# A two-layer block of attention, pooling, S5 scan and gating: another layout of the scan, the readout operators on VectorE, another order of input blocks

## The chip, the cores and the metric

The kernel runs on one core of one Trainium2 chip. The metric is the device time in microseconds of one execution; lower is better. The core has TensorE (matrix products; PE in the views), VectorE (DVE), ScalarE (ACT), GpSimd (POOL), SyncE (SP, which mostly issues DMAs) and 16 DMA engines.

## The reference, cut to what matters

Two layers. Each normalises and modulates its input, projects it once, and hands parts of the projection to four parallel groups (latent attention, pooling mixer, S5 state space, spatial gating), whose outputs are gated, joined and projected back. 1,024 latent and 256 context tokens, width 1,024; the second layer computes outputs for latent tokens only.

```python
h = _ln(x) * (1.0 + scale) + shift
ckv, kr, s5_in, cq, pool_in, su, sv, g = jnp.split(h @ p['w_in'], IN_SPLITS, axis=-1)
...
for d, rev in enumerate((False, True)):
    disc = _s5_discretise(p['lam_re'][d], p['lam_im'][d], p['log_dt'][d],
                          p['s5_b_re'][d], p['s5_b_im'][d])
    hc_r, hc_i = _s5_scan(u_c, disc, rev, None)
    i_end = 0 if rev else nc - 1
    hl_r, hl_i = _s5_scan(u_l, disc, rev, (hc_r[i_end], hc_i[i_end]))
    y_l = y_l + _s5_readout(hl_r, hl_i, p['s5_c_re'][d], p['s5_c_im'][d]).reshape(b, n, BRANCH_W)
...
y = (jnp.concatenate([att_l, pool_l, s5_l, sgu_l], axis=-1) * jax.nn.silu(g)) @ p['w_out']
x_new = (_ln(ALPHA * x + gate * y) * p['ln_g'] + p['ln_b']).astype(x.dtype)
```

The scan is a complex, diagonal recurrence h = a h + b u over all tokens, in both directions, for 16 groups of 64 states.

## The kernel before

**The S5 path.** Tokens are taken in 160 slots of 8, so that the recurrence runs over slots with the 8th power of a, and everything inside a slot is a matrix product. `s5_operators` builds three things per layer from the parameters: the scan-input operators W (on VectorE, function `outer` with engine V, stored to `Ed`), the products inside a slot (kernel K, on TensorE, stored to `Kd`), and the readout operators R (function `outer` with engine P, that is on GpSimd, stored through the tile `bldR` to `Rd`). Their buffers are tiles named op. `s5_states` multiplies the loaded operators (tile Eld) with the tokens and puts the result into the tile H through ScalarE. H holds, for each of two directions, eight pairs of groups, the real and the imaginary part, 161 positions side by side.

`s5_scan` runs in place on H. The 160 positions are five segments of 32; all five are stepped at once, so a step touches positions 32 apart, that is 128 bytes. A step is, for each direction, one multiplication of 160 columns (128 partitions) and two additions of 80, all on VectorE, 31 steps. A table of powers of a is made on GpSimd before. Then a prefix adds the carry of one segment to the next: five small operations per segment and direction, and five larger ones, which stand on GpSimd for three of the four segments of direction 1 (constant PFIX) and else on VectorE. Last an exchange moves half of H to the other partitions, through DRAM: `Xd<-H`, then `H<-Xd`, both issued by GpSimd's queue. `s5_readout` multiplies H by R (tile Rld) and the tokens by M (copied from `Kd`) on TensorE.

**The input blocks.** The input projection is cut into blocks of 128 output columns: gate(i), pl(i) for pooling, su(i) for the spatial unit. For each, SP loads the weight (tile wraw), ScalarE makes its rounded part (whi), VectorE the remainder (wlo), and TensorE does 24 products per chunk of tokens: two with whi and one with wlo for each of eight slices. Layer 0 has three chunks (512, 512, 256 tokens), layer 1 two of 512. Loaded weights, modulation weights (wmod) and operators (Eld, M, Rld) share a ring of three buffers. VectorE evicts gate blocks with one multiplication (G).

**The order.** A list of items per layer sets the program's order: blocks, the states, and the pooled mix. Each block `more(block, n)` advances side work (generators of the operators and of the scan) by a few steps between its chunks; `step(1000)` and `advance(side, 100)` finish side work. Inside that order a scheduler places instructions per engine. Pooling: `pool_mix` forms the window sums of one pooled block, for b = 0 on GpSimd and for b = 1 on VectorE; TensorE then multiplies by w_pool (tp_pool), VectorE evicts. `sgu_prep` loads and transposes the spatial weights (sgw, tp_sgup) in one piece behind gate(4). In attention, for each head and block of queries, VectorE forms maxima (mx), two differences of queries (QA, QB, by `go("m4")`) and a row.

All element-wise operations go through helpers, so their line is the helper's: L131 two-tensor operations, L144 tensor and scalar, L148 both. L152 to L154 are the three products of an input block.

## Time and profile before

| | before |
|---|---|
| median of 3 runs | 1434.23 us (1432.74 to 1434.94) |
| profiled execution | 1430.7 us |
| its span, first to last instruction | 1428.9 us |
| mean granted TensorE clock | 0.950 of 2.4 GHz |
| TensorE busy | 1252.1 us (88%) |
| VectorE busy | 932.5 us (65%) |
| GpSimd busy | 554.7 us (39%) |
| ScalarE busy | 467.6 us (33%) |

A row of a timeline gives start and duration of an instruction, engine, line, operation, the tiles it writes and reads, its shape, and in brackets the idle time of the engine before it with what ended it. A duration is printed with its overlap to the next instruction, so that the distance of two starts is the better price. `x4` means four such instructions in a row, whose duration is that of all. The first layer's scan stretch lies at about 84 to 352 us, the second's at about 820 to 1073 us.

### The profile page before, as it was taken

The page shows a single profiled execution, that of the slowest core. Times are in us where ns is not written, and L with a number is a line of the kernel's source. Part 1 is how long each engine was busy: PE and PEld are TensorE (multiplying, and loading weights), DVE is VectorE, ACT ScalarE, POOL GpSimd, SP SyncE. Part 2 cuts the span into 40 slices and gives each one's busy share as a digit, 9 for nine tenths or more (in the row PEclk, how much of TensorE's full clock was granted, in tenths as well). Part 3 has the DMA queues.
Part 4 walks back from the last instruction along what each step waited for, and adds up shares of the span by engine and source line. Part 5 has one row for each costly group of instructions (what it writes and reads, how often), then busy time and mean ns, then how long its engine had stood idle before and what let it go on. Part 6 is the DMA issues. An engine that isn't in the chain of part 4 may idle for free.

```text
span 1428.9 us, 19998 instructions
## 1 busy us (share of the span) xinstructions
PE 1252.1 (88%) x7556; PEld 962.6 (67%) x7556; DVE 932.5 (65%) x1812; ACT 467.6 (33%) x879; POOL 554.7 (39%) x580
## 2 busy tenths in 40 slices
PE   3877994999999998999999869987599998998997
PEld 1555773779878766666777647765488786665685
DVE  7685399642543566767798882599517456767666
ACT  2341130121244644445243322301213454544300
POOL 2467230500102254665444592224101136756443
PEclk9887997999999989999999979998889999999999
DMA  9435322476320100014123444412662020000421
GB/s 322 135 94 177 115 85 75 117 199 151 83 57 19 45 23 1 1 42 133 48 74 103 100 140 158 138 45 59 135 161 66 11 60 23 30 2 16 150 101 73
DMA packets 124677, 127.31 MB, mean 89 GB/s; under 512 B 40908, under 2 KB 98724, under 8 KB 124582
## 3 DMA queue, kind: packets, MB, share of 16 engines
q1 hardware_dynamic: 118886, 111.86, 26.8%
q0 software_dynamic: 2880, 9.54, 2.8%
q10 hardware_dynamic: 2816, 4.65, 0.9%
q8 instruction: 59, 0.97, 0.3%
q14 instruction: 36, 0.29, 0.1%
HBM read 97.47 MB, written 25.94 MB: 86 GB/s over the span
## 4 chain that ended last, share of the span: by engine, by line
PE 51%; DVE 29%; POOL 6%; issue 6%; DMA 4%; ACT 3%; SPq 1%; DVEq 0%; POOLq 0%; ACTq 0%
PE mm_out L1637 7%; PE mm_sc L1332 6%; PE mm_in L154 6%; PE mm_in L152 6%; PE mm_in L153 6%; DVE H L131 5%; DVE stmp L131 3%; DVE z L148 3%; DVE acc L131 2%; PE av L1415 2%; DVE op L131 2%; PE mm_sc L1374 1%; POOL op L131 1%; DMA M<-Kd 1%; DVE xres L145 1%
## 5 line engine op out<-in xcount | busy, mean ns | idle before, releaser
L154 PE MATMUL mm_in<-hT,wlo 128*128 128x512 f32 (+1 forms) x696 | 264.9, 381 | 26.0 <-DVE wlo L131 26.0
L153 PE MATMUL mm_in<-hT,whi 128*128 128x512 f32 (+1 forms) x696 | 265.1, 381 | 5.0 <-POOL hT L131 2.5
L152 PE MATMUL mm_in<-hT,whi 128*128 128x512 f32 (+1 forms) x696 | 269.0, 388 | 0.4 <-ACT whi L638 0.4
L154 PEld LDWEIGHTS mm_in<-hT,wlo 128*128 128x128 f32 x696 | 136.8, 197 | 53.6 <-DVE wlo L131 28.7
L1637 PE MATMUL mm_out<-wo,yh 128*128 128x512 f32 x576 | 164.2, 398 | 1.8 <-DVE wo L131 1.7
L152 PEld LDWEIGHTS mm_in<-hT,whi 128*128 128x128 f32 x696 | 136.6, 197 | 36.9 <-issue 14.2
L153 PEld LDWEIGHTS mm_in<-hT,whi 128*128 128x128 f32 x696 | 136.5, 196 | 31.4 <-POOL hT L131 5.3
L1637 PEld LDWEIGHTS mm_out<-wo,yh 128*128 128x128 f32 x576 | 107.3, 188 | 29.9 <-DVE wo L131 3.3
L638 ACT CAST whi<-wraw 128x1024 fp32r<-128x1024 f32 x38 | 42.6, 1121 | 194.6 <-PE mm_in L153 146.8
L131 DVE TENSOR_TENSOR wlo<-wraw,whi 128x1024 fp32r<-128x1024 f32 x38 | 58.0, 1530 | 68.0 <-ACT whi L638 61.7
L131 DVE TENSOR_TENSOR acc<-acc,mm_sc 128x512 f32<-128x512 f32 x108 | 74.2, 687 | 42.3 <-PE mm_sc L1332 31.2
L131 POOL TENSOR_TENSOR psum<-pE 128x512 f32<-128x512 f32 (+1 forms) x36 | 47.4, 1318 | 124.2 <-ACT pE L1393 124.1
L1637 PE MATMUL mm_out<-wo,yl 128*128 128x512 f32 x288 | 93.1, 395 | 0.3 <-POOL yl L131 0.3
L131 POOL TENSOR_TENSOR psum<-psum,pL 128x512 f32<-128x512 f32 x64 | 83.2, 1300 | 6.4 <-ACT pL L1393 1.5
L131 DVE TENSOR_TENSOR H<-H,stmp 128x80 f32<-128x80 f32 x248 | 74.6, 355 | 0.8
L144 POOL TENSOR_SCALAR rs_z<-mv_z 128x1 f32<-128x1 f32 x18 | 18.5, 1029 | 119.9 <-DVE mv_z L1669 119.9
L144 POOL TENSOR_SCALAR srs<-smv 128x1 f32<-128x1 f32 x18 | 5.6, 310 | 152.6 <-DVE smv L1065 152.6
L1637 PEld LDWEIGHTS mm_out<-wo,yl 128*128 128x128 f32 x288 | 54.2, 188 | 13.4 <-POOL yl L131 0.8
L131 DVE TENSOR_TENSOR stmp<-a,H 128x160 f32<-128x160 f32 x124 | 53.3, 462 | 14.6 <-POOL pws L131 7.2
L1393 ACT ACTIVATE pE<-mm_sc 128x512 f32<-128x512 f32 x55 | 30.7, 595 | 95.0 <-PE mm_sc L1374 73.7
L1621 ACT CAST yh<-G 128x1024 fp32r<-128x1024 f32 x18 | 18.9, 1052 | 115.1 <-PE mm_out L1637 113.8
L1788 ACT ACTIVATE G<-mm_in 128x512 f32<-128x512 f32 (+1 forms) x40 | 22.2, 555 | 104.1 <-PE mm_in L154 104.0
(361 smaller groups left out, 2789.8 us busy)
## 6 DMA issues: line engine op xcount, KB each, us to landing
wmod<-in_w_mod_dram SPq DMA_DIRECT2D x48, 512.0 KB, 4.3
wraw<-in_w_in_dram SPq DMA_DIRECT2D x36, 512.0 KB, 4.1
wor<-in_w_out_dram SPq DMA_DIRECT2D x16, 512.0 KB, 3.5
s5u<-Sd SPq DMA_DIRECT2D x8, 640.0 KB, 7.3
xd<-z SPq DMA_DIRECT2D x10, 512.0 KB, 2.7
xin<-in_x_dram SPq DMA_DIRECT2D x8, 512.0 KB, 7.6
Ed<-E ACTq DMA_DIRECT2D x16, 256.0 KB, 3.0
Rd<-bldR POOLq DMA_DIRECT2D x16, 256.0 KB, 3.9
```

Of the source, the lines that this page charges most:

```text
L131: return e.tensor_tensor(out=out, in0=a, in1=b, op=op)
L144: return e.tensor_scalar(out=out, in0=a, scalar1=s1, scalar2=None, op0=op0)
L148: return V.scalar_tensor_tensor(out=out, in0=a, scalar=s, in1=b, op0=op0, op1=op1)
L152: T.matmul(out, lhsT=ahi, rhs=bhi, start=start, stop=False)
L153: T.matmul(out, lhsT=ahi, rhs=blo, start=False, stop=False)
L154: T.matmul(out, lhsT=alo, rhs=bhi, start=False, stop=stop)
L638: copy(hi, raw)
L1332: T.matmul(out, lhsT=K[:, e, 128 * kt_:128 * kt_ + 128], rhs=Q[:, f], start=(x == 0 and y == 0), stop=False, skip_group_check=True)
L1393: S.activation(out=p, in_=ps, func=AF.Exp, scale=QSCALE)
L1415: T.matmul(st[v][64 * h:64 * h + 64, 0:n], lhsT=Vt[:, BANKS[i // 2][i % 2], 64 * head:64 * head + 64], rhs=st[v, h]["pt"][i // 2][:, n * ( ...
L1637: T.matmul(a[1][nh], lhsT=y[u][:, k, :], rhs=self.W[k][:, v, 512 * nh:512 * nh + 512], start=(k == 0 and u == 0 and v == 0), stop=(k == KC ...
L1788: S.activation(out=G[ci][:, b, :], in_=ps, func=AF.Silu)
```

## The change

**Readout operators.** The calls of `outer` for R leave GpSimd and the loop over directions. They follow behind the W and K parts, on VectorE, with two buffers (`R` and `R2`, once GpSimd's op1). GpSimd keeps the DMAs `Rd<-bldR`.

**Scan.** H is laid out with the five segments side by side: position of step i and segment s is 5 i + s, 165 positions; direction 1 is stored reversed, so both directions take the same step. A step is one multiplication of 320 columns and two additions of 160. The power table is made on VectorE. The prefix makes first all carries (20 small operations of both directions together and a copy), then 16 operations of 8 x 31 x 4 = 992 columns on VectorE; PFIX is gone. ScalarE writes H, and TensorE reads H in the readout, with a step of 20 bytes.

**Pooling.** `pool_mix` is on VectorE for both blocks.

**Order.** pl(1) and mix(1) follow gate(2) (in layer 1 su(0)), ahead of su(1) and gate(3); before, they stood behind the end of the side work. The side work of the scan is finished behind gate(4) instead of ahead of pl(1). `sgu_prep` is cut in two: loads and transposes ahead of gate(4), the products and copies behind it.

**Attention.** `go("m4")`, which has the two differences of queries, follows the row operations instead of standing ahead of them.

```diff
-NPOS = 161
+NPOS = 165
-PFIX = (1, 2, 3)
...
-            Rv = R.rearrange("p (r c q) -> p r c q", r=2, c=4)
             for c in (slice(0, 4), slice(4, 8)):
                 k0, step = ((7, -1), (0, 1))[d]
                 outer(V, tv_, ld, k0, step, [Bb[:, ri, 8 * d:8 * d + 8, :] for ri in range(2)], c, [w[:, c] for w in W], 1)
-
-                k0, step = ((1, 1), (8, -1))[d]
-                outer(P, tp_, ld, k0, step, [CT[:, ri, 8 * d:8 * d + 8, :] for ri in range(2)], c,
-                      [Rv[:, ri] for ri in range(2)], -1)
-                for ri in range(2):
-                    P.dma_start(Rd[l][:, c, 2 * d + ri, :], Rv[:, ri])
                 yield
-            yield
...
+        for d in range(2):
+            for i, c in enumerate((slice(0, 4), slice(4, 8))):
+
+                k0, step = ((1, 1), (8, -1))[d]
+                Rv = (R, R2)[i].rearrange("p (r c q) -> p r c q", r=2, c=4)
+                outer(V, tv_, 2 * l + d, k0, step, [CT[:, ri, 8 * d:8 * d + 8, :] for ri in range(2)], c,
+                      [Rv[:, ri] for ri in range(2)], -1)
+                for ri in range(2):
+                    P.dma_start(Rd[l][:, c, 2 * d + ri, :], Rv[:, ri])
+                yield
...
         for i in range(1, SEG):
...
+            x = tmp[:, 320 * (i % 2):320 * (i % 2) + 64 * NSEG].rearrange("p (x k o s) -> p x k o s", x=16, k=2, o=2)
+            mul(V, x.rearrange("p x k o s -> p (x k) o s"),
+                a8l.rearrange("p x k o -> p (x k) o").unsqueeze(3).to_broadcast([128, 32, 2, NSEG]),
+                states_at(NSEG * i, [[NPOS, 32], [0, 2], [1, NSEG]]))
+            h = states_at(NSEG * i + NSEG, [[2 * NPOS, 16], [NPOS, 2], [1, NSEG]])
             for k in range(2):
...
+                add(V, h, h, x[:, :, k])
             yield
...
+        for d in range(2):
+            re, im = (T2[:, c, 8 * d:8 * d + 8, 0:w].unsqueeze(3).to_broadcast([128, 8, w, NSEG - 1]) for c in range(2))
+            for o in range(2):
+                own, other = (states_at((16 * d + y) * NPOS + 1, [[2 * NPOS, 8], [0, w], [1, NSEG - 1]]) for y in (o, 1 - o))
+                cur = states_at((16 * d + o) * NPOS + NSEG + 1, [[2 * NPOS, 8], [NSEG, w], [1, NSEG - 1]])
+                mul(V, m, re, own)
+                add(V, cur, cur, m)
+                mul(V, m, im, other)
+                tt(V, cur, cur, m, ALU.add if o else ALU.subtract)
+                yield
...
-                    T.matmul(o, lhsT=R_[:, 1, :], rhs=H[:, 1, pr, g, 1:1 + nr], start=False, stop=False)
+                    T.matmul(ov, lhsT=R_[:, 1, :], rhs=spread(H[:, 1, pr, g, NSLOT - 1:NSLOT], [[-1, nr // SEG], [-NSEG, SEG]]),
+                             start=False, stop=False)
...
-        e = V if b else P
+        e = V
...
-                go("m4")
                 vals(v, w, k, 1)
                 rows(v, h)
+                go("m4")
...
-        items += [more(gate(2), 3)] + ([more(su(0), 3)] if last else []) + [more(su(1), 3), more(gate(3), 3)]
-        items += [lambda: step(1000), lambda: advance(side, 100), more(pl(1), 3), mix(1), more(gate(4), 3)]
-        items += [lambda: step(1000), lambda: advance(side, 100), lambda: sgu_prep(l), begin(s5_readout(l, last))]
+        items += [more(gate(2), 3)] + ([more(su(0), 3)] if last else []) + [mixed, more(pl(1), 3), mix(1), more(su(1), 3)]
+        items += [more(gate(3), 3), mixed, lambda: next(prep), more(gate(4), 3), lambda: next(prep), lambda: step(1000)]
+        items += [begin(s5_readout(l, last))]
```

Three places of the order. First VectorE in layer 0's operators, before; op0 to op4 are the operator buffers, wlo the remainders of weight blocks, dd a part of K:

```order
L131 TENSOR_TENSOR wlo_1002<-wraw_997,whi_1001 128x1024
L131 TENSOR_TENSOR op0_766<-lamT_543,op4_770 128x512
L131 TENSOR_TENSOR wlo_1006<-wraw_999,whi_1005 128x1024
L131 TENSOR_TENSOR op2_768<-op0_766 128x512
L131 TENSOR_TENSOR op0_766<-lamT_543,op4_770 128x512
L620 COPY dd_914<-kt_1116 128x32
L131 TENSOR_TENSOR op0_766<-lamT_543,op4_770 128x512
L131 TENSOR_TENSOR op3_769<-op0_766 128x512
L131 TENSOR_TENSOR op0_766<-lamT_543,op4_770 128x512 x2
L131 TENSOR_TENSOR op2_768<-op0_766 128x512
L131 TENSOR_TENSOR op0_766<-lamT_543,op4_770 128x512 x2
L131 TENSOR_TENSOR wlo_1197<-wraw_1009,whi_1196 128x1024
```

And the same place of VectorE after; the last three of these rows belong to the readout operators:

```order
L130 TENSOR_TENSOR wlo_998<-wraw_991,whi_997 128x1024
L130 TENSOR_TENSOR op2_768<-op0_766 128x512
L130 TENSOR_TENSOR op0_766<-lamT_543,op4_770 128x512 x2
L609 COPY dd_914<-kt_1067 128x32
L130 TENSOR_TENSOR op3_769<-op0_766 128x512
L130 TENSOR_TENSOR op0_766<-lamT_543,op4_770 128x512 x2
L130 TENSOR_TENSOR op2_768<-op0_766 128x512
L130 TENSOR_TENSOR op0_766<-lamT_543,op4_770 128x512 x2
L130 TENSOR_TENSOR op3_769<-op0_766 128x512
L130 TENSOR_TENSOR op0_766<-lamT_543,op4_770 128x512 x2
L130 TENSOR_TENSOR bldR_912<-op0_766 128x4x8x16
L130 TENSOR_TENSOR op0_766<-lamT_543,op4_770 128x512 x2
```

The operators that TensorE transposes next (op2, op3) and the weight remainders keep their order; 24 readout instructions per layer now stand behind them on VectorE, with one wlo among them in layer 0.

Second TensorE in layer 0 where it takes up the first pooled block, before; mm_in_1959 is a chunk of su(1), tp_pool the pooled products, pv the window sums, mm_mod a modulation product:

```order
L153 MATMUL mm_in_1959<-hT0_0_128,whi_1776 128x512
L154 MATMUL mm_in_1959<-hT0_0_128,wlo_1777 128x512
L994 MATMUL tp_pool_1985<-pv_1650,wpool_118 128x512
L994 MATMUL tp_pool_1988<-pv_1650,wpool_118 128x512
L217 MATMUL mm_mod_1795<-wmod_1957,sT_100 32x256
L994 MATMUL tp_pool_1991<-pv_1650,wpool_118 128x256
L217 MATMUL mm_mod_1795<-wmod_1957,sT_100 32x256 x3
L152 MATMUL mm_in_2018<-hT0_1_615,whi_1776 128x512
```

And after; mm_in_1820 is the last chunk of gate(2), mm_in_1881 the first of pl(1):

```order
L152 MATMUL mm_in_1820<-hT0_2_616,whi_1580 128x256
L153 MATMUL mm_in_1820<-hT0_2_616,wlo_1581 128x256
L978 MATMUL tp_pool_1860<-pv_1617,wpool_118 128x512
L978 MATMUL tp_pool_1863<-pv_1617,wpool_118 128x512
L216 MATMUL mm_mod_1735<-wmod_1778,sT_100 32x256
L978 MATMUL tp_pool_1866<-pv_1617,wpool_118 128x256
L216 MATMUL mm_mod_1735<-wmod_1778,sT_100 32x256 x3
L151 MATMUL mm_in_1881<-hT0_0_128,whi_1716 128x512
```

The pooled products of block 0 moved one chunk of 24 products earlier, and the block behind them is now the second pooled block.

Third GpSimd at the end of layer 0's scan, before; stmp, pws and H belong to the prefix, Xd is the exchange buffer in DRAM:

```order
L131 TENSOR_TENSOR stmp_1548<-pws_1547,H0_1442 128x496 x2
L131 TENSOR_TENSOR H0_1442<-H0_1442,stmp_1548 128x16x31
L131 TENSOR_TENSOR H0_1442<-H0_1442,stmp_1548 128x8x31 x2
L851 DMA Xd1_123<-H0_1442 1024x1x161
L851 DMA Xd0_122<-H0_1442 1024x1x161
L853 DMA H0_1442<-Xd0_122 64x16x161
```

And after; pw is a tile of pooling:

```order
L934 MEMSET pw_1907 128x8
L934 MEMSET pw_1907 128x16
L934 MEMSET pw_1907 128x8
L831 DMA Xd1_123<-H0_1442 1024x1x165
L831 DMA Xd0_122<-H0_1442 1024x1x165
L833 DMA H0_1442<-Xd0_122 64x16x165
```

GpSimd has no arithmetic of the scan any more; the exchange's DMAs follow small fills and wait for VectorE alone.

## Rows read from the trace of the kernel before

**Rows 1.** The page: the chain that ended last, shares of the span.

```profile
PE 51%; DVE 29%; POOL 6%; issue 6%; DMA 4%; ACT 3%; SPq 1%; DVEq 0%; POOLq 0%; ACTq 0%
```

**Rows 2.** TensorE's timeline at seven gaps: start, duration, work [idle before, releaser].

```profile
106.71 0.79 PE L154 MATMUL mm_in<-hT,wlo 128*128 128x512 f32 x1 [5.65 <-DVE wlo L131]
...
135.38 1.08 PE L598 MATMUL tp_s5op<-ident,op 128*128 128x128 f32 x4 [9.01 <-DVE op L131]
...
220.40 1.08 PE L217 MATMUL mm_mod<-wmod,sT 128*32 128x256 f32 x8 [6.90 <-DMA wmod<-in_w_mod_dram]
...
243.38 1.22 PE L994 MATMUL tp_pool<-pv,wpool 128*128 128x256 f32 x2 [12.15 <-DVE G L148]
...
852.30 0.58 PE L154 MATMUL mm_in<-hT,wlo 128*128 128x256 f32 x1 [10.33 <-DVE wlo L131]
...
977.80 1.08 PE L245 MATMUL mm_mod<-wmod,sT 128*32 128x256 f32 x8 [8.00 <-DMA wmod<-in_w_mod_dram]
...
1035.41 0.69 PE L1018 MATMUL tp_sgup<-sgw 128*64 128x128 f32 x2 [12.52 <-ACT sgw L1010]
```

**Rows 3.** Stretches: length, busy PE, PEld, DVE, ACT, POOL; granted clock, DMA share.

```profile
107.00:113.00 6.00, 6.00 (x16) 4.65 (x16) 3.39 (x2) 0.00 (x0) 5.90 (x5) 0.54 0.53 159
...
1036.00:1042.00 6.00, 6.00 (x19) 3.36 (x19) 0.74 (x2) 0.00 (x0) 0.00 (x0) 0.50 1.01 273
```

**Rows 4.** The same view, the stretch of layer 0's operators.

```profile
84.00:172.00 88.00, 70.86 (x433) 56.26 (x433) 51.59 (x75) 22.22 (x47) 51.82 (x73) 0.86 0.43 135
```

**Rows 5.** VectorE's timeline in layer 0's operators.

```profile
102.78 3.87 DVE L131 TENSOR_TENSOR wlo<-wraw,whi 128x1024 fp32r<-128x1024 f32 x1
...
136.48 1.22 DVE L131 TENSOR_TENSOR wlo<-wraw,whi 128x1024 fp32r<-128x1024 f32 x1
```

**Rows 6.** VectorE's timeline: two plain operations of different length.

```profile
238.81 0.66 DVE L131 TENSOR_TENSOR sm<-pws,H 128x496 f32<-128x496 f32 x1
...
289.03 1.52 DVE L131 TENSOR_TENSOR p<-pw 128x1311 f32<-128x1311 f32 x1
```

**Rows 7.** VectorE's timeline in layer 0's scan, one direction, then both.

```profile
181.01 0.44 DVE L131 TENSOR_TENSOR stmp<-a,H 128x160 f32<-128x160 f32 x1 [7.04 <-ACT H L758]
181.48 0.64 DVE L131 TENSOR_TENSOR H<-H,stmp 128x80 f32<-128x80 f32 x2
...
192.57 0.82 DVE L131 TENSOR_TENSOR stmp<-a,H 128x160 f32<-128x160 f32 x2
193.29 0.94 DVE L131 TENSOR_TENSOR H<-H,stmp 128x80 f32<-128x80 f32 x4
194.12 0.82 DVE L131 TENSOR_TENSOR stmp<-a,H 128x160 f32<-128x160 f32 x2
```

**Rows 8.** GpSimd's timeline at the exchange, layer 0, then layer 1.

```profile
274.24 1.71 POOL L851 DMA_DIRECT2D Xd<-H  x2 [6.64 <-DVE H L131]
287.83 1.66 POOL L853 DMA_DIRECT2D H<-Xd  x2 [11.89 <-DMA Xd<-H]
...
1007.67 1.69 POOL L851 DMA_DIRECT2D Xd<-H  x2 [6.35 <-DVE H L131]
```

**Rows 9.** TensorE's timeline in layer 0: first state product, first readout product with H.

```profile
171.67 2.57 PE L749 MATMUL tp_s5st<-s5u,Eld 128*64 128x160 f32 x32
...
323.77 0.43 PE L891 MATMUL tp_s5rd<-H,Rld 128*128 128x160 f32 x2
```

**Rows 10.** DMA issues, 260 to 320 us: count, KB each, us to landing.

```profile
H<-Xd POOLq DMA_DIRECT2D x2, 644.0 KB, 10.5
```

**Rows 11.** TensorE's timeline in layer 1: readout's start, first product of the spatial unit.

```profile
1046.45 0.39 PE L154 MATMUL mm_in<-hT,wlo 128*128 128x512 f32 x1
1046.68 0.38 PE L888 MATMUL tp_s5rd<-s5u,M 128*128 128x128 f32 x2
...
1071.78 0.98 PE L1044 MATMUL tp_sgu<-sgw,vnt 128*64 128x128 f32 x14
```

**Rows 12.** VectorE's timeline in attention, one of 16 such places.

```profile
541.52 0.41 DVE L131 TENSOR_TENSOR QA<-qp,QA 64x256 fp32r<-64x256 f32 x1
```

130 lines of the change are left out of this document (50 added, 80 removed).

## The prediction, made before the changed kernel was run

> **What bounds the kernel now.** I read the chain that ended last first: TensorE holds 51% of the span and VectorE 29%, with GpSimd, queues and DMA far behind [rows 1]. So the time is TensorE's work plus the waits that VectorE inflicts on it, and the next view is TensorE's timeline, for its idle gaps. In the stretches that the change touches, in which the scan's operators are built and the scan runs, seven gaps stand out [rows 2]. In layer 0 they are 5.65 and 9.01 us in the operators, 6.90 and 12.15 us in the scan; in layer 1 10.33, 8.00 and 12.52 us. The reader is to see in each row what ended the gap: a low part of a weight block (wlo) or an operator (op) that VectorE delivered late, a gate product G that stood behind the scan on VectorE, a modulation weight whose buffer was freed late, or the sgw copy on ScalarE.
>
> Each gap costs twice. In the 6 us behind the first one TensorE is busy for all 6.00 us at a granted clock of 0.54, in the 6 us behind the last one at 0.50 [rows 3], that is mostly at the lower level (1.2 GHz) after idling. Against full clock, 6 x (1 - clock) is lost: 2.8 and 3.0 us for these two; the five stretches behind the other gaps, in order of time, have clocks of 0.68, 0.65, 0.58, 0.70 and 0.59 in the same view.
>
> Third, VectorE itself. Between 84 and 172 us it is busy 51.59 of 88 us and GpSimd 51.82 [rows 4], and they slow each other: one wlo takes 3.87 us there and 1.22 us when GpSimd is quiet [rows 5]. So GpSimd's readout operators, which nobody needs before the scan has ended, stretch the VectorE work for which TensorE waits.
>
> **Part 1, readout operators to VectorE, behind the others.** GpSimd loses 24 products of 512 columns a layer, VectorE gains them. The price of a plain VectorE operation follows from 0.66 us at 496 columns and 1.52 us at 1311 [rows 6]: 1.055 ns a column and 0.14 us as printed, of which 0.07 overlaps the neighbour; 512 columns are 0.61 us. So the price is 16 x 0.61 plus 8 whose output is written in 32-byte steps. No row of before shows such a write on VectorE; between the plain 0.61 and 0.61 plus 512 x 0.75 ns (the surcharge found in part 2) = 1.0 I take 0.9, near the latter. That is 9.8 + 7.2 = 17 us a layer, 14.6 to 17.8. In layer 0 VectorE idles 88 - 51.6 = 36 us in that stretch and part of its busy time is stretching, so the 17 us and the power table (part 2, 9 us) are covered; without that cover they would delay the scan's start, which TensorE feels only through the states' readout. In layer 1 the states' tile H takes over the operators' buffers, so the state products wait until the last readout operator is made: this is the dearer place. Gone are the gaps 5.65 and 9.01 us, and 2.8 us of low clock behind the first and 6 x (1 - 0.68) = 1.9 us behind the second: **-19.4 us** in layer 0. If only the first goes, it is -8.5. GpSimd keeps the DMA issues, which now stand in no one's way.
>
> **Part 2, the scan.** In the paired steps two multiplications of 160 take 0.72 us (192.57 to 193.29) and four additions of 80 take 0.83 us (to 194.12) [rows 7]: 0.36 and 0.207 each, where the plain price gives 0.236 and 0.151, so the 128-byte step costs 0.7 to 0.8 ns a column. With one direction alone, one multiplication takes 0.47 us to the next start and an addition 0.32, some 0.115 us more each: waiting for the instruction before. After the change a step is one multiplication of 320 and two additions of 160, each dependent on the last, with runs of five neighbours. Without surcharge that is 0.405 + 2 x 0.236 + 3 x 0.115 = **1.22 us**; the bounds are 0.88 (other work fills the latency) and 1.70 (surcharge stays, 640 x 0.75 ns). Against 1.55 us before, 31 steps take 37.9 instead of 48.1 us. I take the end without surcharge, since four of five accesses are neighbours as in the plain rows.
>
> [...]
>
> The prefix is now 16 operations of 992 at 1.11 us, 17.8 us, all on VectorE, and 20 small ones, 3.5 us. For layer 0 VectorE's queue from the first step is: steps 37.9, prefix and small ones 21.3, both pooled blocks at six operations of about 1.5 us [rows 6], 18, five wlo 5.7, gates and the rest some 7: 90 us, an estimate. Before it ran from 181.01 [rows 7] to 274.24 us [rows 8], 93 us. So the scan itself ends hardly earlier; it absorbs GpSimd's prefix and the pooled blocks at no gain and no loss. The start comes later against the state products (about 16 us behind the first of them, which stood at 171.67 us [rows 9]; 9.3 before), since the two directions are merged. The end is then 16 + 90 = 106 us behind the first state product (102.6 before). From there to the exchanged H: 13.6 us to the second DMA (274.24 to 287.83), 0.85 us of issue [rows 8], 10.5 us to landing [rows 10], 25 us: H at 131.
>
> **Part 3, order of blocks.** Before, TensorE wanted H at 323.77 us [rows 9], 152.1 us behind the first state product, though it had landed at 299: TensorE was late, not H. Taking out 6.90 and 12.15 and the low clock behind them (2.1 and 2.5) gives 128.5. New waits: the first pooled products now stand at once behind the second gate block, a chunk of products earlier, and the third needs VectorE to evict, now beside the scan: 4 to 7 us. TensorE arrives at 133 to 135 and H is there at 131. I take 134: **-18 us** for layer 0 (0 if H comes at 152, -23 without new waits).
>
> Layer 1 has 10.33, 8.00 and 12.52 us to lose and 1.8 + 2.5 + 3.0 of low clock: 38.2 us. The check by the other path: VectorE ended at 1007.67 [rows 8]; with the scan's start some 12 us earlier, for the delay at 852.30 is gone, it ends at 995 and H is there at 1020. Before, the first gate product of the spatial unit stood at 1071.78, 25.1 us behind the readout's start at 1046.68 [rows 11]. In the new order TensorE does 53 weight products of the spatial unit and a piece of the gate block ahead of the readout, so that behind it 25.1 - 53 x 0.12 - 24 x 0.23 = 13 us are left (0.23 us is a product of 512 columns, 1046.45 to 1046.68, 0.12 one of 256): 1033. Both give **-38 us**. The bounds: -50 if the smaller gaps between these go too and H is early enough (with H at 1020 TensorE would then wait for it some ten microseconds), -15 if the 17 us of readout operators delay H in full.
>
> The gating preparation in two parts separates the loads and transposes from the products that need the ScalarE copies; this is where the 12.52 us came from, ScalarE having stood behind copies that waited for DMA, and it is counted there. The M copies now reuse scan buffers and wait for the scan's end on ScalarE and SP; queued behind them in layer 1 is one whi, for which TensorE then waits a few microseconds; I cost it at nothing, since H, due later still, is wanted just behind it; without that cover it costs up to 5.
>
> **Part 4, attention.** The two subtractions stand between the maximum and the row: two of 0.41 us [rows 12], some 0.85 with their gaps, at 16 places, 14 us at most. Where the subtracted queries or another releaser are waited for soon after, nothing is gained; I take **-6** (-2 to -9).
>
> **Part 5, what it adds.** The readout reads H with a 20-byte step: 10,240 columns in layer 0 and 8,192 in layer 1. No row of before shows a strided read by TensorE; between 0 and 18,432 x 0.75 ns = 13.8 us I take +3, nearer to nothing, since two products of 160 columns take 0.43 us [rows 9], 1.3 ns a column, so that a read could be 0.75 ns longer beside them. Weight buffers that come free at other times: +3 (0 to 8), by the 8.00 us gap that one of them caused.
>
> **The sum.** -19.4 - 18 - 38 - 6 + 3 + 3 = -75.4 against the profiled execution of 1430.7 us (span 1428.9): 1355.3. The median of the runs is 3.5 us above that execution, so 1358.8; I say **1358**.
>
> **Rivals.**
> - *The surcharge stays on short runs.* Steps cost 1.70 us, the prefix (runs of four) 1.85: 31 x 0.48 + 16 x 0.74 = 27 us more on VectorE a layer. H comes at 158 in layer 0 and TensorE waits 24; in layer 1 all 27 minus a little show: about +45, 1403. For it: rows 7 prove the surcharge. Against it: the step there is 128 bytes for every column. Chance 0.15.
> - *The readout pays in full.* Each column of H that TensorE reads costs VectorE's surcharge on top: 13.8 instead of 3, 1369. Against it: rows 9, as above. Chance 0.10. [...]
> - *The latency is filled.* Steps near 0.9 us; layer 0 stays with TensorE, layer 1 gains another 10, and 5 of the new waits vanish: 1343. Chance 0.10.
> - *The change doesn't relieve layer 1.* The readout operators hold H's buffers, the scan starts where it did: 1381. Chance 0.06.
> - *Slower than before.* The merged scan walks 31 x 640 + 16 x 992 = 35,700 columns a layer on VectorE alone. If each cost 1.25 ns more, half as much again as rows 7 show, the chain grows by 45 us a layer and H decides in both: 1358 + 84 = 1442. It decides from 1.15 ns. Against it: nothing in the trace is so dear. Chance 0.05.
>
> **How the numbers follow.** The forecast has 0.54. The range, 1335 to 1402, takes in the second to fourth rival and half of the first. A measurement of this kernel tells about 0.2% (2.9 us) from no change; only the last rival and the far ends reach that: faster 0.94, same 0.01, slower 0.05.
>
> **What would show it.** The gaps of 5.65 and 9.01 us are absent and wlo takes near 1.2 us in layer 0's operators; a scan step takes 1.1 to 1.3 us and a prefix operation 1.1; TensorE meets the readout's first H product some 20 us earlier against the first state product with no wait above 3 us for H in layer 0, and 0 to 10 in layer 1; readout products keep their durations. The prediction is wrong if TensorE waits tens of microseconds for H, or if a new gap at the pooled products exceeds 10 us.

## The result, and the profile after

The changed kernel took 1389.64 us in the median of four runs (1384.24 to 1395.15), the kernel before 1434.59 us beside it; the ratio is 0.9692 (0.9660 to 0.9723), clearly faster. In a second comparison on one chip, run as a yardstick for the experiments, the same kernel stood at 1384.84 us and 0.9634 (0.9598 to 0.9670). The gain is 45 to 50 us where 76 were forecast. The time lies inside the range, between the fourth rival's figure and the first's.

Two profiled executions of the changed kernel are used: one of 1395.15 us (span 1393.4, the longest of its four runs) and the yardstick's (span 1383.6). All times in this table are starts in TensorE's timeline, subtracted; each stretch ends where the next begins, and only products that write the tile mm_sc are counted as score products.

| stretch | before | after | after, yardstick | forecast for the difference |
|---|---|---|---|---|
| up to layer 0's operators | 84.3 | 83.3 | 83.1 | 0 |
| layer 0's operators, to the first state product | 87.4 | 71.3 | 71.7 | -19.4 |
| states to the first readout product with H | 152.1 | 138.3 | 136.6 | -18 |
| from there to the spatial unit's first product | 27.8 | 36.3 | 36.5 | about +1.7 |
| to the first score product | 128.5 | 131.0 | 129.5 | 0 |
| layer 0's scores, first to last | 177.8 | 184.4 | 184.5 | about -3 |
| to layer 1's operators | 166.3 | 166.3 | 166.3 | 0 |
| layer 1's operators, scan and readout, to the spatial unit | 247.6 | 213.1 | 213.7 | -38, and +1.3 |
| to the first score product | 94.4 | 96.1 | 96.1 | 0 |
| layer 1's scores, first to last | 153.7 | 164.3 | 156.9 | about -3 |
| to the last product | 99.3 | 99.3 | 99.2 | 0 |

The stretches that build and run the scan give what they were to give, within a quarter. Attention, forecast with the wrong sign, and layer 0's readout, forecast too small, take 18 to 26 us back. On the page, the chain that answers [rows 1] has less VectorE and GpSimd and more ScalarE:

```profile
PE 53%; DVE 28%; issue 6%; ACT 5%; DMA 4%; POOL 3%; SPq 0%; DVEq 0%; POOLq 0%; ACTq 0%
```

The stretch of layer 0's operators, which answers [rows 4]; the columns are the length, the busy time of PE, PEld, DVE, ACT and POOL, the granted clock and the DMA share:

```profile
83.00:155.00 72.00, 66.73 (x434) 52.40 (x435) 50.83 (x98) 22.32 (x47) 11.64 (x17) 0.95 0.51 165
```

GpSimd's 51.82 us there have become 11.64, the clock has risen from 0.86 to 0.95, and VectorE, with 23 more instructions in that stretch, is busy for no longer. Its timeline at the weight remainder that took 3.87 us [rows 5], and at the new readout operators:

```profile
95.89 1.22 DVE L130 TENSOR_TENSOR wlo<-wraw,whi 128x1024 fp32r<-128x1024 f32 x1
...
113.70 1.29 DVE L130 TENSOR_TENSOR op<-lamT,op 128x512 f32<-128x512 f32 x2
115.10 1.15 DVE L130 TENSOR_TENSOR bldR<-op 128x512 f32<-128x512 f32 x1
116.28 1.29 DVE L130 TENSOR_TENSOR op<-lamT,op 128x512 f32<-128x512 f32 x2
```

The remainder takes 1.22 us. Two plain products take 1.40 and 1.33 us to the next start, 0.67 to 0.70 each where 0.61 was taken; the write in 32-byte steps takes 1.18 us, more than the 0.9 taken and more than the bound of 1.0. From one such write to the next it is 2.51 us, so eight groups of three take some 20 us a layer, where 17 were forecast (14.6 to 17.8). The scan, against [rows 7]:

```profile
181.33 0.49 DVE L130 TENSOR_TENSOR stmp<-a,H 128x320 f32<-128x320 f32 x1
181.86 0.69 DVE L130 TENSOR_TENSOR H<-H,stmp 128x160 f32<-128x160 f32 x2
182.58 0.49 DVE L130 TENSOR_TENSOR stmp<-a,H 128x320 f32<-128x320 f32 x1
...
241.60 1.19 DVE L130 TENSOR_TENSOR stmp<-pws,H 128x992 f32<-128x992 f32 x1
242.83 1.19 DVE L130 TENSOR_TENSOR H<-H,stmp 128x992 f32<-128x992 f32 x1
244.06 1.19 DVE L130 TENSOR_TENSOR stmp<-pws,H 128x992 f32<-128x992 f32 x1
```

A step takes 181.33 to 182.58, 1.25 us (forecast 1.22, before 1.55), a prefix operation 1.23 us (1.11 without the wait for the one before it, which the forecast left out there). Runs of five and of four neighbours pay no surcharge: they print 0.49 us at 320 columns and 1.19 at 992, where the plain price from [rows 6] gives 0.48 and 1.19.

What TensorE meets behind the scan is in the next rows, of its own, SP's, ScalarE's and GpSimd's timelines in layer 0:

```profile
288.48 1.43 PE L868 MATMUL tp_s5rd<-s5u,M 128*128 128x160 f32 x4 [6.28 <-ACT M L848]
...
271.31 0.33 SPq L241 DMA_DIRECT2D wmod<-in_w_mod_dram  x1
271.73 7.75 SPq L841 DMA_DIRECT2D M<-Kd  x8
...
281.15 0.69 ACT L848 COPY M<-M 128x128 f32<-128x128 f32 x2 [12.10 <-DMA M<-Kd]
...
259.35 0.79 POOL L831 DMA_DIRECT2D Xd<-H  x1 [6.31 <-DVE H L130]
271.01 1.65 POOL L833 DMA_DIRECT2D H<-Xd  x2 [10.87 <-DMA wmod<-in_w_mod_dram]
```

The scan is done at 259.35, 104.8 us behind the first state product (forecast 106). H goes back at 271.01 and lands 11 us after its issue, at about 283 (forecast 131 us behind the first state product, here 128). TensorE was there at 288.48 - 6.28 = 282.2, 127.6 us behind the first state product and earlier than forecast (134), and then waited not for H but for M: the M loads stand on SP behind a modulation weight that got its buffer at 271.31. The size of this wait varies: in the yardstick's execution TensorE comes 129.7 us behind the first state product, and the same wait is 2.77 us:

```profile
287.23 0.81 PE L868 MATMUL tp_s5rd<-s5u,M 128*128 128x160 f32 x4 [2.77 <-ACT M L848]
```

The readout products with H, before in [rows 9] 0.43 us for two of 160 columns:

```profile
297.11 0.72 PE L872 MATMUL tp_s5rd<-H,Rld 128*128 128x160 f32 x2
297.65 0.64 PE L874 MATMUL tp_s5rd<-H,Rld 128*128 128x128 f32 x2
298.11 0.33 PE L877 MATMUL tp_s5rd<-H,Rld 128*128 128x32 f32 x2
298.27 0.52 PE L868 MATMUL tp_s5rd<-s5u,M 128*128 128x160 f32 x2
...
1003.71 0.70 PE L872 MATMUL tp_s5rd<-H,Rld 128*128 128x128 f32 x2 [3.26 <-DMA H<-Xd]
```

They take 0.72 printed, 0.54 us to the next start, and the six of one pair of operators 297.11 to 298.27, 1.16 us, at a granted clock of 1.00. In layer 1 TensorE waits 3.26 us for H, as the forecast had it (0 to 10).

Last, layer 1's scores. First two waits of the kernel before, then the wait that stands in their place after and the next of its kind, in TensorE's timeline:

```profile
1194.53 0.65 PE L1435 MATMUL tp_sm<-psum,ones 128*64 128x256 f32 x4 [0.88 <-DVE row L148]
...
1201.56 0.41 PE L1354 MATMUL tp_mx<-ident,acc 128*128 128x128 f32 x2 [0.96 <-DVE acc L131]
```

```profile
1157.45 0.41 PE L1341 MATMUL tp_mx<-ident,acc 128*128 128x128 f32 x2 [2.11 <-DVE acc L130]
...
1198.54 0.41 PE L1341 MATMUL tp_mx<-ident,acc 128*128 128x128 f32 x2 [2.12 <-DVE acc L130]
```

The stretch behind the second of these waits, and then the whole of layer 1's scores, before and after, as rows of stretches:

```profile
1200.00:1208.00 8.00, 8.00 (x37) 6.21 (x37) 3.19 (x6) 3.15 (x6) 3.60 (x4) 0.50 0.21 66
...
1166.00:1320.00 154.00, 139.89 (x1033) 100.14 (x1031) 105.75 (x173) 76.91 (x149) 93.19 (x80) 1.00 0.06 20
...
1120.00:1284.00 164.00, 149.71 (x1027) 107.41 (x1025) 107.55 (x171) 76.55 (x149) 91.69 (x80) 0.93 0.06 19
```

Two waits of 0.9 us have become one of 2.11 us at 1157.45. Behind the next such wait, 2.12 us at 1198.54, TensorE is busy for the whole 8 us at a granted clock of 0.50. In the kernel before, products of 512 columns start 0.427 us apart at that clock (twelve steps from 107.30 to 112.42 us), 1.2 columns a ns (1.2 GHz, if a cycle takes a column), and 0.23 us apart at 1.00 (116.22 to 120.66). Over the whole of these scores the clock was 1.00 before and is 0.93 after.

### The profile page after: what moved, and what is told of

The parts are those of the page before. It is cut to its first block, busy times and chain, and to the rows that moved or that the text cites. A ratio compares the mean times of both kernels' runs of the same rounds, so it can differ in the third digit from the quotient of the medians.

```text
span 1393.4 us, 19654 instructions
## 1 busy us (share of the span) xinstructions
PE 1273.8 (91%) x7556; PEld 979.7 (70%) x7556; DVE 897.7 (64%) x1636; ACT 475.3 (34%) x879; POOL 413.9 (30%) x418
## 3 DMA queue, kind: packets, MB, share of 16 engines
q1 hardware_dynamic: 118886, 111.86, 27.8%
## 4 chain that ended last, share of the span: by engine, by line
PE 53%; DVE 28%; issue 6%; ACT 5%; DMA 4%; POOL 3%; SPq 0%; DVEq 0%; POOLq 0%; ACTq 0%
PE mm_out L1624 7%; PE mm_sc L1319 6%; PE mm_in L152 5%; PE mm_in L151 5%; PE mm_in L153 5%; PE av L1402 4%; DVE acc L130 3%; DVE H L130 3%; DVE z L147 3%; DVE op L130 2%; DVE stmp L130 2%; DVE xres L144 1%; PE mm_sc L1361 1%; PE tp_s5rd L872 1%; PE tp_sc L1319 1%
## 5 line engine op out<-in xcount | busy, mean ns | idle before, releaser
L152 PE MATMUL mm_in<-hT,whi 128*128 128x512 f32 (+1 forms) x696 | 262.1, 377 | 4.5 <-POOL hT L130 3.4
L151 PE MATMUL mm_in<-hT,whi 128*128 128x512 f32 (+1 forms) x696 | 264.8, 382 | 0.1
L153 PE MATMUL mm_in<-hT,wlo 128*128 128x512 f32 (+1 forms) x696 | 260.3, 375 | 0.0
L151 PEld LDWEIGHTS mm_in<-hT,whi 128*128 128x128 f32 x696 | 133.3, 192 | 34.9 <-issue 11.9
L152 PEld LDWEIGHTS mm_in<-hT,whi 128*128 128x128 f32 x696 | 133.4, 192 | 31.2 <-POOL hT L130 6.4
L153 PEld LDWEIGHTS mm_in<-hT,wlo 128*128 128x128 f32 x696 | 133.3, 192 | 24.2 <-issue 1.6
L130 DVE TENSOR_TENSOR wlo<-wraw,whi 128x1024 fp32r<-128x1024 f32 x38 | 48.4, 1274 | 49.5 <-ACT whi L637 49.4
L1624 PEld LDWEIGHTS mm_out<-wo,yl 128*128 128x128 f32 x288 | 54.2, 188 | 13.4 <-POOL yl L130 0.8
L130 DVE TENSOR_TENSOR H<-H,stmp 128x160 f32<-128x160 f32 (+1 forms) x140 | 59.3, 424 | 3.9
L1319 PEld LDWEIGHTS mm_sc<-QA,KT 96*128 96x128 f32 x372 | 56.2, 228 | 7.1 <-issue 6.9
L1319 PE MATMUL mm_sc<-QA,KT 96*128 96x256 f32 x372 | 61.1, 325 | 0.0
```

Source lines behind the costliest of these rows:

```text
L130: return e.tensor_tensor(out=out, in0=a, in1=b, op=op)
L151: T.matmul(out, lhsT=ahi, rhs=bhi, start=start, stop=False)
L152: T.matmul(out, lhsT=ahi, rhs=blo, start=False, stop=False)
L153: T.matmul(out, lhsT=alo, rhs=bhi, start=False, stop=stop)
L1319: T.matmul(out, lhsT=K[:, e, 128 * kt_:128 * kt_ + 128], rhs=Q[:, f], start=(x == 0 and y == 0), stop=False, skip_group_check=True)
L1624: T.matmul(a[1][nh], lhsT=y[u][:, k, :], rhs=self.W[k][:, v, 512 * nh:512 * nh + 512], start=(k == 0 and u == 0 and v == 0), stop=(k == KC ...
```

## The experiments

Theory after the comparison: (A) the later place of the two query differences costs time, by merging waits and by the low clock behind the longer one; (B) the 20-byte step doubles the readout's reads; (C) the operators and the scan do what the forecast said, and M, not H, sets layer 0's readout. The rivals are named with each run. Medians are compared through the ratio to the kernel before, which ran beside each set; the changed kernel's two ratios, 0.9692 and 0.9634, also show how far two sets differ.

**The changed kernel again**, without an edit.

> The changed kernel itself, as the yardstick for the other three on the same chip. Its four times so far lie between 1384 and 1395 us. If the low-clock stretches in attention are a fixed consequence of its order of instructions, its mean clock in layer 1's attention is again near 0.93 and the times again lie within about 10 us; if they are chance, the profile shows another number of them.

Measured: 1384.84 us (1378.99 to 1385.51), ratio 0.9634. Layer 1's scores took 156.9 us instead of 164.3. One wait of this run in TensorE's timeline, and then the stretches behind it and of the whole scores:

```profile
1194.65 0.41 PE L1341 MATMUL tp_mx<-ident,acc 128*128 128x128 f32 x2 [2.12 <-DVE acc L130]
```

```profile
1196.00:1204.00 8.00, 7.91 (x63) 5.88 (x62) 5.31 (x10) 4.31 (x9) 5.35 (x5) 1.00 0.26 82
1118.00:1275.00 157.00, 142.57 (x1030) 101.79 (x1028) 107.70 (x173) 76.57 (x148) 92.27 (x79) 0.98 0.06 19
```

The wait is the same 2.12 us, and here the clock did not fall behind it. So these waits in attention are fixed by the order of instructions and whether the clock falls behind one of them is not: the second expectation was right. That may be why this kernel's runs spread over 16 us.

**The query differences back.**

```diff
                 maxima(v, h)
+                go("m4")
                 vals(v, w, k, 1)
                 rows(v, h)
-                go("m4")
```

> The changed kernel with the two differences of queries back ahead of the row operations. Theory A: the later place merges two short waits of TensorE (0.9 and 0.9 us) into one of 2.1 us at the maxima, and behind such a wait TensorE runs at 1.2 GHz for some 8 us. Then the two attention stretches, 185 and 164 us in the profile of the changed kernel, return to about 178 and 154 us, layer 1's attention has a granted clock of 1.00, and the kernel is 10 to 17 us faster than the changed one. Rival B: the low clock has another origin (how the stretch is entered), and the place of the two differences costs or saves nothing: within 4 us of the changed kernel. Forecast's own reckoning: 6 us slower than the changed kernel.

Measured: 1376.71 us, ratio 0.9582 (0.9545 to 0.9618) against 0.9634 of the yardstick on the same chip, 8 us faster; the two intervals overlap a little, the four times of each do not. Layer 1's scores took 154.8 us with no wait above 1.74 us, layer 0's 182.5. The whole stretch in layer 1:

```profile
1114.00:1269.00 155.00, 141.35 (x1030) 101.38 (x1029) 105.57 (x173) 76.62 (x150) 92.94 (x79) 0.99 0.06 20
```

The direction is that of theory A, the size below its 10 to 17 us, since the yardstick's own profile shows a smaller loss in layer 1 than the first one. Layer 0's scores don't return to 178 us: of the 6.7 us that they lost, 2.0 come back. They have the waits of the kernel before again, 16.1 us over 0.3 us in all against 16.5, but a clock of 0.93 against 0.95. So in these profiles most of layer 0's loss has another origin, which stays open, and waits shorter than 2 us don't always leave the clock at full either: in the kernel before none of layer 0's is longer than 1.48 us, and behind those of 0.52 to 1.10 us the 8 us from 552 on have 0.57.

**The same edit alone, on the kernel before.**

```diff
                 maxima(v, h)
-                go("m4")
                 vals(v, w, k, 1)
                 rows(v, h)
+                go("m4")
```

> The kernel before with this one edit alone, the two differences of queries behind the row operations. Theory A: 10 to 17 us slower than before (about 1445 to 1451 us), with waits near 2.1 us at the maxima and low clock behind them. Rival B: within 4 us of before. Forecast's own reckoning: 6 us faster.

Measured: 1442.73 us, ratio 1.0064 (1.0029 to 1.0099), 9 us slower, over a spread of 1435 to 1455. The forecast's sign is excluded, and so is no effect. Three waits in layer 1 in TensorE's timeline, and then the stretches behind them:

```profile
1207.39 0.30 PE L1354 MATMUL tp_mx<-ident,acc 128*128 128x128 f32 x1 [2.12 <-DVE acc L131]
...
1249.88 0.30 PE L1354 MATMUL tp_mx<-ident,acc 128*128 128x128 f32 x1 [2.11 <-DVE acc L131]
...
1290.59 0.45 PE L1354 MATMUL tp_mx<-ident,acc 128*128 128x128 f32 x1 [2.10 <-DVE acc L131]
```

```profile
1208.00:1216.00 8.00, 8.00 (x38) 5.63 (x35) 2.77 (x6) 3.15 (x6) 3.72 (x4) 0.53 0.00 0
1250.00:1258.00 8.00, 7.91 (x60) 5.83 (x61) 5.13 (x10) 3.50 (x7) 5.43 (x6) 1.00 0.21 66
1291.00:1299.00 8.00, 8.00 (x54) 5.61 (x53) 4.25 (x8) 3.14 (x6) 2.78 (x4) 0.82 0.00 0
```

The three waits are alike within 0.02 us; behind them the clock is 0.53, 1.00 and 0.82. TensorE's idle time in layer 1's scores is 13.1 us in 11 gaps over 0.3 us, before it was 13.4 in 17: nothing was gained in idle time there, it was only gathered, and the loss of 7 us in this stretch is the low clock (0.95 over the whole of it, before 1.00).

**The readout by runs.** The columns are taken as H lies in memory, so the step moves to the writing side, in PSUM.

```diff
-                    ov = o.rearrange("p (a b) -> p a b", b=SEG)
-                    T.matmul(ov, lhsT=R_[:, 1, :], rhs=spread(H[:, 1, pr, g, NSLOT - 1:NSLOT], [[-1, nr // SEG], [-NSEG, SEG]]),
+                    ov = o.rearrange("p (a b) -> p b a", b=SEG)
+                    T.matmul(ov, lhsT=R_[:, 1, :], rhs=spread(H[:, 1, pr, g, NSLOT - 1:NSLOT], [[-NSEG, SEG], [-1, nr // SEG]]),
...
-                    T.matmul(ov[:, 0:NSEG - 1], lhsT=R_[:, 0, :], rhs=spread(H[:, 0, pr, g, 1:2], [[1, NSEG - 1], [NSEG, SEG]]),
+                    T.matmul(ov[:, :, 0:NSEG - 1], lhsT=R_[:, 0, :], rhs=spread(H[:, 0, pr, g, 1:2], [[NSEG, SEG], [1, NSEG - 1]]),
...
-                        T.matmul(ov[:, NSEG - 1], lhsT=R_[:, 0, :], rhs=spread(H[:, 0, pr, g, 0:1], [[NSEG, SEG]]),
+                        T.matmul(ov[:, :, NSEG - 1], lhsT=R_[:, 0, :], rhs=spread(H[:, 0, pr, g, 0:1], [[NSEG, SEG]]),
```

> The changed kernel with the readout's columns taken in the order in which H lies in memory (runs of four or five neighbours), so that the step of 32 columns is on the writing side, in PSUM. Theory: reading H with a 20-byte step doubles a column's time on TensorE at full clock (0.135 to 0.27 us for 160 columns), 8.6 us in layer 0 and 7.5 us in layer 1. If only reading is slow, the readout products return to 0.135 us a 160 columns and the kernel is 10 to 16 us faster than the changed one; if reading in runs of five still pays for each new line, part of it stays (0.16 to 0.2 us); if a PSUM write with a step costs as much, nothing changes (0.27 us, within 3 us).

Measured: 1367.83 us, ratio 0.9514 (0.9474 to 0.9554), 17 us faster than the yardstick. The edit brings slightly more than the 10 to 16 us of the first expectation. The products, again at full clock:

```profile
296.60 0.43 PE L872 MATMUL tp_s5rd<-H,Rld 128*128 128x160 f32 x2
296.88 0.38 PE L874 MATMUL tp_s5rd<-H,Rld 128*128 128x128 f32 x2
297.10 0.31 PE L877 MATMUL tp_s5rd<-H,Rld 128*128 128x32 f32 x2
297.24 0.52 PE L868 MATMUL tp_s5rd<-s5u,M 128*128 128x160 f32 x2
```

Six take 0.64 us instead of 1.16, two of 160 columns print 0.43 us as in [rows 9]. Over 16 such groups that is 8.3 us in layer 0, and the stretch from H to the spatial unit shrinks from 36.3 to 28.2; in layer 1 from 20.4 to 14.4. So the whole added cost of the readout in the changed kernel is the strided read, and reading in runs of five pays nothing (0.28 us to the next start for two of 160 columns, 0.27 in the kernel before). Here the products write PSUM with a step of 128 bytes, and they take 0.43 us as before: this write costs nothing.

**Readout operators back on GpSimd**, inside the loop over directions; the rest of the change stays.

```diff
                 outer(V, tv_, ld, k0, step, [Bb[:, ri, 8 * d:8 * d + 8, :] for ri in range(2)], c, [w[:, c] for w in W], 1)
+
+                k0, step = ((1, 1), (8, -1))[d]
+                Rv = R.rearrange("p (r c q) -> p r c q", r=2, c=4)
+                outer(P, R2, ld, k0, step, [CT[:, ri, 8 * d:8 * d + 8, :] for ri in range(2)], c,
+                      [Rv[:, ri] for ri in range(2)], -1)
...
-                outer(V, tv_, 2 * l + d, k0, step, [CT[:, ri, 8 * d:8 * d + 8, :] for ri in range(2)], c,
-                      [Rv[:, ri] for ri in range(2)], -1)
```

> The changed kernel with the readout operators back on GpSimd, inside the loop over directions as before; all else stays changed. Theory: GpSimd and VectorE slow each other there, so wlo takes 2 to 4 us again in the operators, the gaps of about 5.6 and 9 us in layer 0 and of about 10 us in layer 1 return, and the kernel is 20 to 30 us slower than the changed one (about 1405 to 1415 us). Rival: TensorE's later waits (for M and H) absorb what is lost early, within 6 us of the changed kernel.

Measured: 1408.43 us, ratio 0.9822 (0.9786 to 0.9857): 1.3 to 1.9 points behind the changed kernel, 19 to 27 us. TensorE's gaps and VectorE's weight remainder:

```profile
106.78 0.79 PE L153 MATMUL mm_in<-hT,wlo 128*128 128x512 f32 x1 [5.33 <-DVE wlo L130]
...
851.76 0.58 PE L153 MATMUL mm_in<-hT,wlo 128*128 128x256 f32 x1 [10.31 <-DVE wlo L130]
...
102.85 3.88 DVE L130 TENSOR_TENSOR wlo<-wraw,whi 128x1024 fp32r<-128x1024 f32 x1
```

The gaps of [rows 2] and the 3.87 us of [rows 5] are back nearly to the digit, except that the second gap in layer 0 is now 2.65 and 1.87 us. Layer 0's operators take 82.8 us (71.3 and 71.7 in the changed kernel). In layer 1 the operators lose 13.5 us and the whole way to the spatial unit only 8: the wait for H, 3.26 us, is gone, and some 5 us come back, so that the rival is right for a part there.

**The old order of items**, with everything else changed.

```diff
-        items += [more(gate(2), 3)] + ([more(su(0), 3)] if last else []) + [mixed, more(pl(1), 3), mix(1), more(su(1), 3)]
-        items += [more(gate(3), 3), mixed, lambda: next(prep), more(gate(4), 3), lambda: next(prep), lambda: step(1000)]
-        items += [begin(s5_readout(l, last))]
+        items += [more(gate(2), 3)] + ([more(su(0), 3)] if last else []) + [more(su(1), 3), more(gate(3), 3)]
+        items += [lambda: step(1000), lambda: advance(side, 100), more(pl(1), 3), mix(1), more(gate(4), 3)]
+        items += [lambda: step(1000), lambda: advance(side, 100), lambda: next(prep), lambda: next(prep), begin(s5_readout(l, last))]
```

> The changed kernel with the old order of items: su(1), gate(3), then all side work finished, then pl(1), the second pooled mix and gate(4), then the gating preparation in one piece. Theory: the order is worth the gaps of 6.9 and 12 us in layer 0 and 8 and 12.5 us in layer 1 less the new waits, so this kernel is 15 to 30 us slower than the changed one. Rival: those gaps came from the slow scan and GpSimd's prefix, and the new scan removes them by itself; then it is within 6 us of the changed kernel, or faster, as VectorE's queue has 9 us less ahead of the scan's end.

Measured: 1390.20 us, ratio 0.9696 (0.9654 to 0.9738), against 0.9692 and 0.9634: between no difference and some 9 us, and so clear of the 15 to 30 of the theory. The rival holds, as far as two sets can be compared. In layer 0 the first readout product with H comes 134.1 us behind the first state product (138.3 and 136.6 with the new order) and no gap above 2.1 us is left in the scan's stretch; in layer 1 the stretch to the spatial unit takes 217.7 us (213.1 and 213.7), with 4.55 us of the gap that was 12.52, so that the two layers give and take about 4 us each:

```profile
988.31 0.69 PE L1004 MATMUL tp_sgup<-sgw 128*64 128x128 f32 x2 [4.55 <-ACT sgw L994]
```

Layer 0's scan ends 92.3 us behind the first state product here (104.8 with the new order), since VectorE's queue has no second pooled block ahead of that end. There is no wait for M above 1 us: H went back at 259.10, the M loads start at 274.17, and they land after 3.3 us where they took 9.7 (7.5 in the yardstick).

**Everything but the scan**: the kernel before with readout operators on VectorE, new order, both pooled mixes on VectorE, preparation in two parts and the query differences moved; H's layout, steps, GpSimd's prefix and the readout as before. The edits are those of the change's diff without `s5_states`, `s5_scan` and `s5_readout`.

> The kernel before with all parts of the change but the scan: readout operators on VectorE, new order of items, both pooled mixes on VectorE, gating preparation in two parts, the two differences of queries moved; layout of H, steps, prefix on GpSimd and readout as before. If the parts add up, the scan's part is worth what is left of the changed kernel's gain: readout operators about 21 us, order about 5, attention -8, so that this kernel stands near 1415 to 1420 us, 30 us behind the changed one. If the old scan and the new order get in each other's way (GpSimd's prefix, the gap of 12 us at the pooled products), it is no faster than before. If the new scan brings nothing net, since the readout's strided reads take it back, this kernel is within 5 us of the changed one.

Measured: 1413.14 us, ratio 0.9848 (0.9821 to 0.9875). Three of TensorE's gaps:

```profile
207.18 1.22 PE L994 MATMUL tp_pool<-pv,wpool 128*128 128x256 f32 x2 [5.42 <-DVE G L148]
...
263.94 1.22 PE L994 MATMUL tp_pool<-pv,wpool 128*128 128x512 f32 x1 [7.02 <-DVE pv L131]
...
989.29 1.22 PE L994 MATMUL tp_pool<-pv,wpool 128*128 128x512 f32 x1 [14.45 <-DVE pv L131]
```

The scan, with its prefix and its table of powers on VectorE, is worth 1.6 to 2.1 points, 22 to 31 us, net of what its readout loses, near what the first expectation had. What this kernel gains over the one before, 21 us, is what the readout operators bring by themselves (19 to 27); with the old scan the new order, the pooled mixes and the query differences together bring about nothing. And the new order with the old scan has waits at the pooled products again (5.42, 7.02, 14.45 us): VectorE, still with 1.47 us a step and its part of the prefix, delivers what these products need late. No run moves the pooled mix of block 0 alone, so its part stays open.

**Both edits together**: query differences back and readout by runs; the diffs are those above. It was run in two sets, the second time beside the readout by runs alone.

> The changed kernel with two edits: the two differences of queries back ahead of the row operations, and the readout's columns by runs. If the two effects are independent, 8 + 17 us faster than the changed kernel, about 1360 us (ratio to before 0.945 to 0.950); if TensorE then only waits longer for H in layer 1, some 5 us of that is lost.

Measured: 1363.92 us, ratio 0.9519 (0.9480 to 0.9557), short of the 0.945 to 0.950 of two independent effects. Against the readout by runs in the set before, 0.9514, no gain is seen.

> The changed kernel with the readout's columns by runs, once more, as the yardstick for the next two on the same chip: ratio to before about 0.951.

Measured: 1367.47 us, ratio 0.9523 (0.9500 to 0.9546).

> Columns by runs and the two differences of queries back ahead of the row operations. If the later place costs 8 us as in the pair without the other edit, the ratio to before is 0.945 or 0.946; if the effect hangs on how attention is entered, it is 0.951 as for the previous kernel.

Measured: 1362.93 us, ratio 0.9494 (0.9467 to 0.9520). On one chip the query differences are worth 4.5 us here, half of the 8 and 9 us of the other pairs, and the two intervals overlap. The sign is the same in the three pairs that ran side by side; beside the readout by runs it is not clear of noise, and the size is open between 4 and 9 us. This is the fastest kernel of the study, 1.5 to 2% ahead of the changed one.

**Against the wait for M**, on top of both edits: the raw M tiles in another ring of buffers.

```diff
-        M0 = [wr("M0"), wr("M0")]
+        M0 = [xs("M0"), xs("M0")]
...
-                src = M0[a].rearrange("p (s q h) -> p s q h", s=4, q=16)
+                src = M0[a][:, 0:1024].rearrange("p (s q h) -> p s q h", s=4, q=16)
```

> As the previous one, and in addition the raw M tiles in the ring of the 1,312-column tiles instead of the ring that weight blocks use. Theory: in layer 0 the 6.28 us that TensorE waits for the M copies come from the M loads, which stand on SP until a weight buffer is free (271.7 us, 12 us behind the scan's end); with other buffers they are there when TensorE comes, the wait goes and some 2 us of low clock behind it, 6 to 9 us faster than the previous kernel. Rival: H lands at 283 us or later and TensorE waits for it instead, 0 to 3 us.

Measured: 1372.70 us, ratio 0.9576 (0.9544 to 0.9608), 9 us slower than without it; neither expectation had that. There was also less to gain than the theory took: 6.28 us stand in one execution of the changed kernel, while the two profiles of this kernel without the edit have 2.45 and 2.73 us. The wait for M is gone and stands elsewhere, at a modulation weight and at the operators Rld:

```profile
284.69 1.08 PE L244 MATMUL mm_mod<-wmod,sT 128*32 128x256 f32 x8 [6.58 <-DMA wmod<-in_w_mod_dram]
...
289.40 0.87 PE L872 MATMUL tp_s5rd<-H,Rld 128*128 128x160 f32 x2 [2.90 <-DMA Rld<-Rd]
```

**The same wait, another way**: four pieces through the small ring, loaded from ScalarE's queue.

```diff
-        M0 = [wr("M0"), wr("M0")]
-        for s in range(8):
-            D.dma_start(M0[s // 4][:, 256 * (s % 4):256 * (s % 4) + 256], Kd[l][(7 - s) * 16:(7 - s) * 16 + 128, :])
+        for a in range(4):
+            M0 = s2("M0")
+            for s in range(2):
+                S.dma_start(M0[:, 256 * s:256 * s + 256], Kd[l][(7 - 2 * a - s) * 16:(7 - 2 * a - s) * 16 + 128, :])
...
```

> As the previous one, and the raw M tiles in four pieces through the ring of 512-column tiles, loaded from ScalarE's queue, so that neither the weight ring nor the weight loads on SP hold them. Theory: in layer 0 the M products no longer wait 6.28 us and the first readout product with H comes at 128 to 132 us behind the first state product instead of 138, set by H's landing; 4 to 8 us faster than the previous kernel. Rival: the copies hold up gate evictions and whi on ScalarE, and TensorE loses as much there (0, or slower).

Measured: 1375.46 us, ratio 0.9586 (0.9566 to 0.9607), 12.5 us slower than both edits alone on the same chip, as the rival had it. ScalarE loads, waits, copies, and loads the next piece, and TensorE's wait for M has grown:

```profile
267.87 0.44 ACT L848 COPY M<-M 128x128 f32<-128x128 f32 x1 [12.42 <-DMA M<-Kd]
...
290.36 0.64 PE L868 MATMUL tp_s5rd<-s5u,M 128*128 128x160 f32 x1 [11.16 <-ACT M L848]
```

The first load, issued at 256, was there only 12 us later; in this stretch the exchange of H, modulation weights and M are under way together (in the changed kernel the queues that carry them hold 22.5 and 43.0% of the time of the 16 DMA engines between 245 and 300 us), and in the changed kernel an M load takes 9.7 us from issue to landing where it took 3.0 before (7.5 in the yardstick). That the exchange's traffic sets the wait fits two rows more: with the old order of items, where the exchange was over before they started, the loads took 3.3 us, and in this run the pair issued at 284.11, behind the exchange, could be copied 2.1 us later. It is still not shown, since no run takes the exchange alone away.

## Why the prediction was right or wrong

**Right in direction and range, too hopeful by 27 to 32 us.** Step by step:

- *Readout operators to VectorE* (-19.4 us in layer 0): right. The operators' stretch lost 16.1 us; both gaps are absent, wlo takes 1.22 us. The run with them back on GpSimd loses 19 to 27 us over both layers. The price on VectorE was too low, some 20 us a layer against 17, mainly by the 32-byte write (1.18 us against 0.9); in layer 0 VectorE's idle time covered it.
- *Scan* (1.22 us a step, 1.11 us a prefix operation, end at 106 us): right, 1.25, 1.23 and 104.8; the prefix left out the 0.115 us of waiting that the step had in. The first rival, the surcharge on short runs, fell. The statement that the scan absorbs GpSimd's prefix at no gain was too modest about what a shorter queue does for others, next point.
- *Order of blocks* (-18 in layer 0, -38 in layer 1): the sizes were near, -13.8 to -15.5 and, with the readout's loss of 6 us taken out, about -40. The cause was wrong. The gaps of 6.90, 12.15, 8.00 and 12.52 us were put down to the order of blocks; the run with the old order and the new scan has lost nearly all of them, and the run with the new order and the old scan has three of 5.42, 7.02 and 14.45 us. They went with the scan; whether its steps or GpSimd's part of the prefix did it, no run separates. (The ScalarE copy of the spatial weights, which ended the 12.52, went ahead of gate(4) with the transposes and not behind it as the section on the change has it.) In layer 0 the step that failed was "I cost it at nothing" for the M copies: their loads waited on SP behind a weight load, and TensorE waited 6.28 us, in the yardstick 2.77, where only layer 1 had been looked at. TensorE's arrival, 127.6 and 129.7 us, was better than the 134 forecast, so that the two errors nearly cancel.
- *Readout reads* (+3, bounds 0 and 13.8): the mechanism was the second rival's, and it happened in full: 8.3 and 6.0 us by the stretches, 17 us between the medians. The argument for the small value was that the read could hide beside the product's own 1.3 ns a column. That figure came from a printed duration, which has the overlap in it: in the kernel before, the next group starts 0.27 us behind the two products, 0.84 ns a column, hardly more than the surcharge of 0.75 ns itself. The rows show 0.27 us instead of 0.135 for 160 columns; nothing was hidden.
- *Attention* (-6, bounds -2 and -9): wrong in sign, outside its bounds. The count took each wait for a row as idle time that would vanish. In layer 1 it moved to the next maximum, with the same sum (13.1 us against 13.4), and came in pieces of 2.1 us, behind which the clock can fall. Three pairs give 4 to 9 us slower. The stretches of the scores lost 10 to 17 us in all, so a part of the loss, above all in layer 0, is not from this edit and stays unexplained.
- *Weight buffers* (+3): there in the M wait, which is one of them.

The mis-sized terms are attention, -6 forecast and +4 to +9 by the pairs, and the readout, +3 forecast and about +14 by the stretches: 21 to 26 of the 27 to 32 us. The rest lies in layer 0's operators (3 to 4 us), in the open part of its scores, and in runs that differ by several microseconds. That the order of blocks came out near its number is luck: its gaps went, but by the scan.

## What to carry to other kernels

A gap in front of a product is not a budget by itself: ask which engine's queue was late. Here the gaps went with a faster queue under either order, and not with the new order alone, so that a gap is counted once, for the queue. Count where idle time gathers and not only how much there is: in layer 1's scores, with the same idle time in sum, waits of 0.9 us left TensorE at full clock where three of 2.1 us did not always do so. When a layout is turned for one reader, price the other readers from the access pattern, from the distance of two starts and not from a printed duration, and try the turn on the side that writes to PSUM.
